# DeltaNet's z projection moves from the per-unit projections to the seven-product stage

## The chip, the cores and the metric

The kernel runs on one core of a Trainium2 chip. The time is the device time of one execution in microseconds (us). The engines are named as in the profile: PE (TensorE, matrix products), PEld (its weight loads), DVE (VectorE), ACT (ScalarE), POOL (GpSimd) and SP (SyncE, which here only issues DMAs). SPq and ACTq are the DMA issues on SP's and ACT's queues.

## The reference, cut to what matters

One layer, 512 tokens, 2048 channels, everything in float32:

```python
u = _rmsnorm(h, norm_w)
proj = jnp.matmul(u, w_in)            # 2048 x 20528
...
h_a = _mlstm_chunkwise(ml_q, ml_k, ml_v, i_pre, logf)      # 8 heads
h_a = _rmsnorm(h_a) * ml_norm_w * sigmoid(ml_o) * silu(ml_z)
qkv = _causal_conv_silu(dn_qkv, dn_conv_w)                  # width 4
h_b = _gated_delta_chunkwise(dq, dk_, dv_, beta, g)         # 16 heads of 128
h_b = _merge_heads(_rmsnorm(h_b, dn_norm_w)) * silu(dn_z)
y_a, y_b = h_a @ w_out[:2048], h_b @ w_out[2048:]
return sigmoid(gate_a) * y_a + sigmoid(gate_b) * y_b        # then residual, final norm
```

DeltaNet solves, per head and chunk, a unit lower triangular system, and then runs a chain over the chunks in which each state depends on the one before. The change concerns `dn_z`, the 2048 columns whose SiLU gates DeltaNet's normalised head outputs.

## The kernel before, in words

Each float32 operand is split into a high and a low part (`split_hi` on ACT, `split_lo` on DVE), and each product is three matmuls: high x high, high x low, low x high. The order of PE's instructions is the order in which the program is written; the other engines' and the DMA queues' order is made by a scheduler from dependences and priorities (`urgent`, `high_priority`, `behind`: not before the newest weight split).

The work outside the big products is written as generators that are advanced by `tick()`: after every step of a product loop, `tick` runs each generator whose due time has come, and `yield n` lets n steps pass. A step is six matmuls of 512 columns (twelve of 256 in `proj_tm`). So a PE instruction in a generator has a fixed place among the matmuls of the projections, and PE stands still there if its operand is not ready.

The stages are these.

1. Front. x is normalised and transposed into `uh`, `ul` (channels on partitions). Meanwhile the first mLSTM q and k blocks are projected and two blocks of output gates (`narrow_gates`). `u_sums` makes the sums of quarters of u that the next stage needs: POOL adds, ACT and DVE split, all in one tile `X`.
2. Seven-product stage, `seven`, nine blocks given by `SEVEN`. A block multiplies u by two times 512 columns of `w_in` with seven products in place of eight, in the manner of Strassen and Winograd: groups A and B of eight K steps each, with four and three products a step. `prep_sums` and `prep_pair` make and split the weights' sums. Blocks of kind z hold 512 columns each of mLSTM's z and o, kind v mLSTM's v, kind g output gates. `SINK` holds what is done with each kind's results: they come out token-major (tokens on partitions), pass an activation, and are stored to DRAM.
3. Units, in the order of `UNITS`: eight of DeltaNet (two heads each) and three of mLSTM, the first mLSTM unit (`ml_first`) running beside the first of them. `dn_unit` projects K, Q, V and z with `proj_cm`, 16 steps each, 64 in all; the results come channel-major. `conv_silu` and `silu_end` follow on ACT and DVE; `turn` transposes a tile in 32x32 blocks on DVE and by DMA through DRAM. `dn_front_k` makes the decay matrix and the triangular system and solves 32x32 blocks of it on DVE in 62 short instructions (L866, L868); the result goes through DRAM (`xd`, `tt`) and is transposed to `tn`. `dn_back`, started 9 steps after the last projection, combines the blocks on PE (its first product, L923, reads `tn`) and starts two `dn_chain`s, one per head, each some 20 steps long. At its end a chain normalises the head's outputs (`os`), turns them channel-major, and `gated` multiplies by the norm's weight and by `g`, the SiLU of z, on DVE, 13 steps later (`TURN`), and stores to `h_d`.
4. An mLSTM unit projects Q and K in 32 steps and runs `ml_prep`, `ml_rec` and `ml_fin` for two heads beside the following units. `ml_rec` scales `kw` on DVE just ahead of the products that read it (L1087, L1098).
5. Output: more gates, then `w_out` for mLSTM's part, then for DeltaNet's. `load_h` loads `hm_d` (kept in 32x32 blocks, scaled by the norm's weight when it is split) and `h_d` (channel-major, scaled already).

Buffers that the change's order touches: `wk` tiles have rings, shared by unit kinds: `g` 4, `kq` 4, `ke` 4, `aq` 4, `dm` 2, `to` 2; PSUM has three `pj`, three `wk` and two `o` banks. The weight loads of a unit run up to four tiles ahead (`RAHEAD`), the splits three (`SAHEAD`).

Of the kernel before, what the change touches and what calls it, by code (L numbers as in the profile page):

```python
# [8 lines left out]
F32 = mybir.dt.float32  # L9
# [23 lines left out]
KLAST = 4  # L33
TURN = 13
QWAIT = 9
# [21 lines left out]
def hybrid_body(  # L57
# [321 lines left out]
    def u_sums():  # L379
        for i in range(KH):  # L380
            uf, sf = X[:, 0, :, :], X[:, 1, :, :].rearrange("p a (b n) -> p (a b) n", n=HP)
            V.tensor_tensor(out=uf, in0=uh[:, 2 * i:2 * i + 2, :].bitcast(F32), in1=ul[:, 2 * i:2 * i + 2, :].bitcast(F32),
                            op=ALU.add)
            a11, a21, a12, a22 = uf[:, 0, 0:HP], uf[:, 0, HP:S], uf[:, 1, 0:HP], uf[:, 1, HP:S]
            G.tensor_tensor(out=sf[:, 0], in0=a21, in1=a22, op=ALU.add)
            G.tensor_tensor(out=sf[:, 1], in0=sf[:, 0], in1=a11, op=ALU.subtract)
            G.tensor_tensor(out=sf[:, 2], in0=a11, in1=a21, op=ALU.subtract)
            G.tensor_tensor(out=sf[:, 3], in0=a12, in1=sf[:, 1], op=ALU.subtract)
            yield 3
            for hi, lo, src in ((suh[:, i], sul[:, i], sf[:, 0:3]), (s4h[:, i], s4l[:, i], sf[:, 3])):  # L390
                A.copy(hi, src)
                V.tensor_tensor(out=lo, in0=src, in1=hi.bitcast(F32), op=ALU.subtract)
            yield 2

# [169 lines left out]
    def seven(n0, kind, c1, c2):  # L564
# [6 lines left out]
        def product(n, m):  # L571
            g, i = "AB"[n // KH], n % KH
            ps = ((m6, m1, m5, m7) if g == "A" else (m1, m5, m7))[m]
            hi, lo = partq[n0 + n][m]
            for t in range(2):
                ah, al = LHS[g][m](i, slice(t * P, (t + 1) * P))
                T.matmul(ps[t], ah, hi, start=(g == "A" and i == 0), stop=False, skip_group_check=True)  # L577
                T.matmul(ps[t], ah, lo, start=False, stop=False, skip_group_check=True)  # L578
                T.matmul(ps[t], al, hi, start=False, stop=(i == KH - 1), skip_group_check=True)  # L579
                if i == KH - 1 and ends[g][m] is not None:  # L580
                    ends[g][m](t)
            tick()

        N = 2 * KH
        for n in range(N - 2):
            prep_sums(n0 + n + 1)
            prep_pair(n0 + n + 1)
            load_quad()
            if n == N - 3:

                prep_sums(n0 + n + 3)
            for m in range(4 if n < KH else 3):
                if n == N - 3 and m == 2:
                    prep_sums(n0 + N - 1)
                    prep_pair(n0 + N - 1)
                product(n, m)

        load_quad()
        last = n0 + N == len(quads)
        for n, m in ((N - 2, 0), (N - 2, 1), (N - 1, 0), (N - 1, 1), (N - 2, 2), (N - 1, 2)):  # L600
            if (n, m) == (N - 1, 0):
                prep_pair(n0 + N)
                load_quad()
            if last and (n, m) == (N - 1, 1):
                limit[0] = len(plan)
                prepare(nfront - 1)
            product(n, m)
# [32 lines left out]
    def sink_z(c1, c2, m1, m5, m7, last):  # L640
# [31 lines left out]
        def end7(t):  # L672
# [3 lines left out]
        return end1, end5, end7  # L676

    SINK = {"g": sink_flat(lambda c, col: tg_d[c, :, col - GATE:col - GATE + NO], AF.Tanh, 0.5),
            "v": sink_flat(lambda c, col: v_d[c, :, col - ML_V:col - ML_V + NO], AF.Copy, 1.0),
            "z": sink_z}  # L680

# [72 lines left out]

    def silu2(ps, dst):
        th = wk.tile([P, S], F32, tag="th", name="thz", bufs=3)
        with urgent():
            A.copy(dst, ps)
        with urgent():
            A.activation(th, ps, AF.Tanh, scale=0.5)  # L760
        V.scalar_tensor_tensor(out=dst, in0=th, scalar=1.0, in1=dst, op0=ALU.add, op1=ALU.mult)

    def token_norms(pk, dst):
# [13 lines left out]
    def travel(o, dst, out):  # L777
# [10 lines left out]
        with behind("A") if out else urgent(2):  # L788
            q.dma_start(dst, d.rearrange("(n j) r a c -> (j r) n (a c)", n=NC))
        yield 1  # L790

    def gated(hn, w, g, kt):
        with behind("V"):
            V.scalar_tensor_tensor(out=g, in0=hn.rearrange("p c t -> p (c t)"), scalar=w, in1=g, op0=ALU.mult,
                                   op1=ALU.mult)
        nc.sync.dma_start(h_d[kt], g)
        yield 1
# [164 lines left out]
    def dn_chain(j, hs, kq, u):  # L962
# [7 lines left out]
        for c in range(NC):  # L970
# [18 lines left out]
            if c < NC - 1:  # L989
# [3 lines left out]
                with urgent():  # L993
                    if st is None:
                        V.tensor_copy(sn, pst)
                    else:
                        V.scalar_tensor_tensor(out=sn, in0=st, scalar=ge[:, c:c + 1], in1=pst,
                                               op0=ALU.mult, op1=ALU.add)
# [14 lines left out]
        with urgent():  # L1013
            V.tensor_tensor(out=os_, in0=po, in1=bc(rsd, P), op=ALU.mult)
        turn(os_, os_, True)
        start(gated(os_, normc[:, 32:33], u["g"][j], h), TURN)

    def dn_unit(p):
        hs = (2 * p, 2 * p + 1)
        dcol = p * NB  # L1020
        u = {"aq": [], "qt": [], "ke": [], "vs": [], "g": [], "dm": []}
        kq = [wk.tile([P, 2, S], F32, tag="kq", name=f"kq{h}", bufs=4) for h in hs]
# [16 lines left out]
        for j in range(2):  # L1039
# [3 lines left out]
            start(silu_end(vt.rearrange("p c t -> p (c t)"), (vt, vt)), 4 + 3 * j)  # L1043
        ps = proj_cm(DN_Z + dcol)
        for j in range(2):
            g = wk.tile([P, S], F32, tag="g", name="gz", bufs=4)
            silu2(ps[j], g)
            u["g"].append(g)
        start(dn_back(hs, kq, u), 9)

    def ml_prep(j, hs, kq, u):
# [26 lines left out]
        u["em"].append((w, we, de, qi))  # L1078

    def ml_rec(j, hs, kq, u):  # L1080
        h = hs[j]
# [3 lines left out]
        kw = u["kw"][j]  # L1085
        with behind("V"):
            V.tensor_tensor(out=kw, in0=kw, in1=bc(we, P), op=ALU.mult)  # L1087
        sq = wk.tile([P, NC], F32, tag="sq", name="sq")
        c1 = None
        for c in range(NC):  # L1090
# [57 lines left out]
    def ml_start(hs, kq, u):  # L1148
        for j in range(2):
            kw = wk.tile([P, NC, P], F32, tag="ke", name="kw", bufs=4)  # L1150
# [12 lines left out]
    def ml_first(hs, kq, u):  # L1163
# [4 lines left out]
        yield 4  # L1168
        with behind("V"):
            ml_start(hs, kq, u)  # L1170
        yield 5
        yield from ml_both(hs, kq, u)
# [23 lines left out]
    def load_h(base, step):  # L1196
        for k in range(KT):
            raw = wp.tile([P, S], F32, tag="wr", name="hr", bufs=NRAW)
            if base:
                nc.sync.dma_start(raw, h_d[k])  # L1200
                split_hi(hh[base][:, k, :], raw)
                split_lo(hl[base][:, k, :], raw, hh[base][:, k, :])
            else:

                w = normc[:, 16 + k:17 + k]
                nc.sync.dma_start(raw.rearrange("p (n t) -> p n t", n=NC),
                                  hm_d[k].rearrange("(n j) r a c -> (j r) n (a c)", n=NC))
                A.activation(hh[base][:, k, :], raw, AF.Copy, scale=w)
                V.scalar_tensor_tensor(out=hl[base][:, k, :], in0=raw, scalar=w, in1=hh[base][:, k, :].bitcast(F32),
                                       op0=ALU.mult, op1=ALU.subtract)  # L1210
            yield step
# [149 lines left out]
```

## Time and profile before

| | us |
|---|---|
| median of 3 runs | 2276.9 (2273.74 to 2278.14) |
| the profiled execution | 2278.73 |
| its span, first to last instruction | 2276.9 |
| front, to the first seven-product matmul | 136.4 |
| seven-product stage, 9 blocks | 136.4 to 842.0 |
| units | 842.0 to 1844.6 |
| output | 1844.6 to 2276.9 |

The granted clock of PE is 0.994 of full speed over the span. In a group's row stand the line, engine, operation, tiles, shape and count, then busy us, the mean ns of one, and the engine's idle time ahead of them with what ended it. A row of waits has who waited for whom, us in total, times, the longest. A timeline row has start, length, engine, line, operation and tiles, and in brackets the idle time before it. A row of stretches has the stretch, its length, the busy time and count of PE, PEld, DVE, ACT and POOL, PE's granted clock, the share of the DMA engines and GB/s.

### The profile page before, as it was taken

Reading aid. Unit: us, or ns where it says so; the run is one execution under the profiler, and the core shown is the slowest. Engines: PE = TensorE matmul, PEld = TensorE weight load, DVE = VectorE, ACT = ScalarE, POOL = GpSimd, SP = SyncE. Lnnn points to the kernel's source line nnn. Section 1 sums busy time; section 2 is a strip of 40 time slices with the busy share of each in tenths; the row PEclk is TensorE's granted clock in tenths of the full one; section 3 lists DMA queues with packets and bytes.
Section 4 is the critical chain, followed back from the end, with each engine's and each line's share of the span. In section 5 each row is a group of like instructions: output and inputs, shape, how many; then the busy total and the mean of one; then the engine's idle time right before and its main releaser. Section 6 shows DMA issues by size and latency. Waiting matters only on the chain.

```text
span 2276.9 us, 32977 instructions
## 1 busy us (share of the span) xinstructions
PE 2218.0 (97%) x11600; PEld 1858.0 (82%) x11600; DVE 1507.5 (66%) x2725; ACT 893.3 (39%) x1776; POOL 248.3 (11%) x325
## 2 busy tenths in 40 slices
PE   7999999999999999999999999999999999999998
PEld 5888888778778778788888888888888899978886
DVE  5967798777777757776496846867376855334445
ACT  4434444444444443343343434434334334232223
POOL 0500000000000001211021202212022100000111
PEclk9999999999999999999999999999999999999999
DMA  5366666667767757557565746658366556764333
GB/s 157 88 190 188 212 195 213 195 197 232 225 186 221 244 180 201 132 120 197 121 165 121 185 124 155 149 121 204 100 159 144 129 144 201 243 206 149 115 116 131
DMA packets 503464, 384.50 MB, mean 169 GB/s; under 512 B 238337, under 2 KB 402402, under 8 KB 503298
## 3 DMA queue, kind: packets, MB, share of 16 engines
q1 hardware_dynamic: 406018, 333.03, 52.5%
q10 hardware_dynamic: 97280, 49.37, 7.4%
q8 instruction: 91, 1.49, 0.3%
q14 instruction: 75, 0.61, 0.1%
HBM read 309.86 MB, written 72.42 MB: 168 GB/s over the span
## 4 chain that ended last, share of the span: by engine, by line
PE 75%; DMA 9%; DVE 8%; issue 3%; SPq 2%; ACT 1%; POOL 0%; ACTq 0%; DVEq 0%; POOLq 0%
PE pj L249 12%; PE pj L250 11%; PE pj L251 11%; PE ps L578 7%; PE ps L577 6%; PE ps L579 6%; PE py L1295 3%; PE py L1296 3%; PE py L1294 3%; DVE wl L138 3%; DMA wr<-in_w_in_dram 2%; DMA wr<-t_d 2%; PE pjt L264 2%; PE pjt L266 2%; PE pjt L267 2%
## 5 line engine op out<-in xcount | busy, mean ns | idle before, releaser
L138 DVE TENSOR_TENSOR wl<-wr,wh 128x512 fp32r<-128x512 f32 (+1 forms) x624 | 487.2, 786 | 346.0 <-ACT wh L135 336.0
L135 ACT CAST wh<-wr 128x512 fp32r<-128x512 f32 (+1 forms) x624 | 415.6, 669 | 760.3 <-PE pj L250 351.8
L249 PE MATMUL pj<-uh,wh 128*128 128x512 f32 x1280 | 531.1, 415 | 3.2 <-ACT yp L740 3.2
L251 PE MATMUL pj<-uh,wl 128*128 128x512 f32 x1280 | 501.8, 392 | 0.0
L250 PE MATMUL pj<-ul,wh 128*128 128x512 f32 x1280 | 501.3, 392 | 0.0
L251 PEld LDWEIGHTS pj<-uh,wl 128*128 128x128 f32 x1280 | 241.1, 188 | 53.0
L249 PEld LDWEIGHTS pj<-uh,wh 128*128 128x128 f32 x1280 | 242.0, 189 | 49.0 <-ACT yp L740 4.0
L250 PEld LDWEIGHTS pj<-ul,wh 128*128 128x128 f32 x1280 | 242.1, 189 | 43.1
L578 PE MATMUL ps<-wl,uh 128*128 128x512 f32 x432 | 170.6, 395 | 7.1 <-DVE wl L138 7.1
L577 PE MATMUL ps<-wh,uh 128*128 128x512 f32 x432 | 169.6, 393 | 2.5 <-DVE X L558 2.3
L579 PE MATMUL ps<-wh,ul 128*128 128x512 f32 x432 | 168.3, 390 | 0.0
L578 PE MATMUL ps<-wl,suh 128*128 128x512 f32 x432 | 168.1, 389 | 0.0
L577 PE MATMUL ps<-wh,suh 128*128 128x512 f32 x432 | 168.1, 389 | 0.0
L579 PE MATMUL ps<-wh,sul 128*128 128x512 f32 x432 | 168.1, 389 | 0.0
L264 PE MATMUL pjt<-wh,uh 128*128 128x256 f32 x512 | 149.1, 291 | 4.5 <-ACT tgs L696 2.7
L266 PE MATMUL pjt<-wl,uh 128*128 128x256 f32 x512 | 146.7, 287 | 0.4 <-DVE wl L138 0.4
L267 PE MATMUL pjt<-wh,ul 128*128 128x256 f32 x512 | 146.4, 286 | 0.0
L135 ACT CAST wh<-ts 128x512 fp32r<-128x512 f32 x144 | 88.9, 617 | 144.3 <-DVE ts L533 106.5
L135 ACT CAST wh<-t 128x1024 fp32r<-128x1024 f32 x72 | 75.8, 1053 | 160.7 <-PE ps L579 91.2
L138 DVE TENSOR_TENSOR wl<-ts,wh 128x512 fp32r<-128x512 f32 x144 | 98.2, 685 | 23.5 <-ACT wh L135 23.5
L138 DVE TENSOR_TENSOR wl<-t,wh 128x1024 fp32r<-128x1024 f32 x72 | 88.0, 1223 | 33.6 <-ACT wh L135 33.2
L578 PEld LDWEIGHTS ps<-wl,uh 128*128 128x128 f32 x432 | 81.1, 188 | 31.0 <-DVE wl L138 15.6
(286 smaller groups left out, 3691.8 us busy)
## 6 DMA issues: line engine op xcount, KB each, us to landing
wr<-in_w_in_dram SPq DMA_DIRECT2D x712, 256.0 KB, 3.5
wr<-in_w_out_dram SPq DMA_DIRECT2D x128, 256.0 KB, 3.1
t_d<-ts ACTq DMA_DIRECT2D x72, 256.0 KB, 3.7
wr<-t_d SPq DMA_DIRECT2D x72, 256.0 KB, 4.0
tgl<-tg_d SPq DMA_DIRECT2D x24, 256.0 KB, 3.6
xt<-in_x_dram SPq DMA_DIRECT2D x8, 512.0 KB, 7.4
v<-v_d SPq DMA_DIRECT2D x8, 512.0 KB, 5.9
gb<-rows_d SPq DMA_DIRECT2D x16, 256.0 KB, 4.1
```

The lines of the kernel that those rows point to most:

```text
L135: newest["A"] = A.copy(hi, src).ins
L138: newest["V"] = V.tensor_tensor(out=lo, in0=src, in1=hi.bitcast(F32), op=ALU.subtract).ins
L249: T.matmul(ps[j], hi[:, k, wsl], uh[:, kt, :], start=(kt == 0), stop=False)
L250: T.matmul(ps[j], hi[:, k, wsl], ul[:, kt, :], start=False, stop=False)
L251: T.matmul(ps[j], lo[:, k, wsl], uh[:, kt, :], start=False, stop=(kt == KT - 1))
L264: T.matmul(o, uh[:, kt, tsl], hi[:, k, :], start=(kt == 0 and c % 2 == 0), stop=False, skip_group_check=True)
L266: T.matmul(o, uh[:, kt, tsl], lo[:, k, :], start=False, stop=False, skip_group_check=True)
L267: T.matmul(o, ul[:, kt, tsl], hi[:, k, :], start=False, stop=(kt == KT - 1), skip_group_check=True)
L577: T.matmul(ps[t], ah, hi, start=(g == "A" and i == 0), stop=False, skip_group_check=True)
L578: T.matmul(ps[t], ah, lo, start=False, stop=False, skip_group_check=True)
L579: T.matmul(ps[t], al, hi, start=False, stop=(i == KH - 1), skip_group_check=True)
L1294: T.matmul(ps[c], hh[base][:, kt, tsl], hi[:, 0, :], start=(kt == 0), stop=False)
```

## The change

DeltaNet's z leaves `dn_unit`: the projection, `silu2` and `gated` go, and a unit has 48 steps. `SEVEN` gets two blocks of kind s, 1024 columns of z each, between kinds z and v (11 blocks). Their sink computes the SiLU (a copy and a tanh on ACT, one gating operation on DVE) and stores token-major to `gz_d`. A chain loads its head's part of `gz_d` on SP at its second chunk; POOL multiplies the normalised outputs by it, before they are turned; the turned blocks stay in `h_d` as they are, and `load_h` applies the norm's weight for both branches. `dn_back` starts 17 steps after V, where it started 9 after z.

Other steps move: `u_sums` uses two buffers and splits one round after the sums are made; `prep_sums` for the next block's first weights comes four products later; `scale_kw` is called a step before the first head's recurrence, and for the second head inside the first's; mLSTM's recurrence yields 3 in place of 4; `ml_first` starts its two heads five steps apart.

```diff
 SEVEN = ([("z", ML_Z + c, ML_O + c) for c in range(0, D, NO)]
+         + [("s", DN_Z + c, DN_Z + c + NO) for c in range(0, D, 2 * NO)]
          + [("v", ML_V + c, ML_V + c + NO) for c in range(0, D, 2 * NO)]
...
-    h_d = dr.tile([KT, P, S], F32, tag="hd", name="h_d")
+    h_d = dr.tile([KT, 16, BS, 4, BS], F32, tag="hd", name="h_d")
+    gz_d = dr.tile([NC, P, D], F32, tag="gzd", name="gz_d")
...
-        cols = (DN_K, DN_Q, DN_V, DN_Z) if kind == "d" else (ML_Q, ML_K)
+        cols = (DN_K, DN_Q, DN_V) if kind == "d" else (ML_Q, ML_K)
...
     def u_sums():
-        for i in range(KH):
...
-            yield 3
-            for hi, lo, src in ((suh[:, i], sul[:, i], sf[:, 0:3]), (s4h[:, i], s4l[:, i], sf[:, 3])):
-                A.copy(hi, src)
-                V.tensor_tensor(out=lo, in0=src, in1=hi.bitcast(F32), op=ALU.subtract)
-            yield 2
+        for i in range(KH + 1):
+            if i < KH:
+                sums(i)
+            yield 2
+            if i:
+                sf = sfs[i - 1]
+                for hi, lo, src in ((suh[:, i - 1], sul[:, i - 1], sf[:, 0:3]), (s4h[:, i - 1], s4l[:, i - 1], sf[:, 3])):
+                    A.copy(hi, src)
+                    V.tensor_tensor(out=lo, in0=src, in1=hi.bitcast(F32), op=ALU.subtract)
+            yield 3
...
+    def sums(i):
+        uf = sbp.tile([P, 2, NO], F32R, tag="w2h", name="uf", bufs=2).bitcast(F32)
+        sf = sfs[i] = X[:, i % 2, :, :].rearrange("p a (b n) -> p (a b) n", n=HP)
...
             load_quad()
-            if n == N - 3:
-
-                prep_sums(n0 + n + 3)
...
         for n, m in ((N - 2, 0), (N - 2, 1), (N - 1, 0), (N - 1, 1), (N - 2, 2), (N - 1, 2)):
+            if (n, m) == (N - 2, 1):
+                prep_sums(n0 + N)
...
+    def sink_s(c1, c2, m1, m5, m7, last):
+
+        def late(z, c, col):
+            th = spare(True)
+            with behind("A"):
+                A.activation(th, z, AF.Tanh, scale=0.5)
+            with behind("V"):
+                V.scalar_tensor_tensor(out=z, in0=th, scalar=1.0, in1=z, op0=ALU.add, op1=ALU.mult)
+            yield 2
+            with behind("A"):
+                nc.scalar.dma_start(gz_d[c, :, col - DN_Z:col - DN_Z + NO], z)
...
-    def gated(hn, w, g, kt):
-        with behind("V"):
-            V.scalar_tensor_tensor(out=g, in0=hn.rearrange("p c t -> p (c t)"), scalar=w, in1=g, op0=ALU.mult,
-                                   op1=ALU.mult)
-        nc.sync.dma_start(h_d[kt], g)
-        yield 1
...
             T.matmul(po[:, c, :], aq[:, c, 1, :], w, start=(st is None), stop=True)
+            if c == 1:
+                g = wk.tile([P, NC, P], F32, tag="g", name="gz", bufs=4)
+                nc.sync.dma_start(g, gz_d[:, :, h * P:(h + 1) * P].rearrange("c p n -> p c n"))
...
-        turn(os_, os_, True)
-        start(gated(os_, normc[:, 32:33], u["g"][j], h), TURN)
+        G.tensor_tensor(out=os_, in0=os_, in1=g, op=ALU.mult)
+        yield 2
+        turn(os_, h_d[h], True)
...
-        ps = proj_cm(DN_Z + dcol)
-        for j in range(2):
-            g = wk.tile([P, S], F32, tag="g", name="gz", bufs=4)
-            silu2(ps[j], g)
-            u["g"].append(g)
-        start(dn_back(hs, kq, u), 9)
+        start(dn_back(hs, kq, u), 17)
...
+    def scale_kw(j, u):
+        kw, we = u["kw"][j], u["em"][j][1]
+        with behind("V"):
+            V.tensor_tensor(out=kw, in0=kw, in1=bc(we, P), op=ALU.mult)
...
             if c == NC - 2:
+                if j == 0:
+                    scale_kw(1, u)
...
-            yield 4
+            yield 3
...
         for j in range(2):
             yield from ml_prep(j, hs, kq, u)
+        yield 5
+        scale_kw(0, u)
+        yield 1
...
-        with behind("V"):
-            ml_start(hs, kq, u)
-        yield 5
+        for j in range(2):
+            with behind("V"):
+                ml_start(hs, kq, u, (j,))
+            yield 5
...
-            if base:
-                nc.sync.dma_start(raw, h_d[k])
-                split_hi(hh[base][:, k, :], raw)
-                split_lo(hl[base][:, k, :], raw, hh[base][:, k, :])
...
+            w = normc[:, 32:33] if base else normc[:, 16 + k:17 + k]
+            nc.sync.dma_start(raw.rearrange("p (n t) -> p n t", n=NC),
+                              (h_d if base else hm_d)[k].rearrange("(n j) r a c -> (j r) n (a c)", n=NC))
```

More of the change, by code (lines that the diff above doesn't have):

```diff
@@ L579, in product @@
                 T.matmul(ps[t], al, hi, start=False, stop=(i == KH - 1), skip_group_check=True)
-                if i == KH - 1 and ends[g][m] is not None:
+                if i == KH - 1:
                     ends[g][m](t)
@@ L676, in sink_z, with out_, end5, end7 @@
         return end1, end5, end7
+    def sink_s(c1, c2, m1, m5, m7, last):
[8 more added lines that the diff above has]
+                nc.scalar.dma_start(gz_d[c, :, col - DN_Z:col - DN_Z + NO], z)
+        def out_(ps, t, col, wait):
+            z = spare(False)
+            with urgent(3):
+                A.copy(z, ps)
+            start(late(z, t, col), wait + 4 * t)
+        def end5(t):
+            add(m5[t], U1[t], m5[t])
+            out_(m5[t], t, c2, 5)
+        def end7(t):
+            add(U1[t], U1[t], m7[t])
+            start(late(U1[t], 2 + t, c1), 12 + 4 * t)
+            start(late(C22[t], 2 + t, c2), 14 + 4 * t)
+        return (lambda t: out_(m1[t], t, c1, 4)), end5, end7
     SINK = {"g": sink_flat(lambda c, col: tg_d[c, :, col - GATE:col - GATE + NO], AF.Tanh, 0.5),
             "v": sink_flat(lambda c, col: v_d[c, :, col - ML_V:col - ML_V + NO], AF.Copy, 1.0),
-            "z": sink_z}
+            "z": sink_z, "s": sink_s}
     def lead():
@@ L753, in silu_end @@
         yield 1
[L755 to L761, printed above, removed]
     def token_norms(pk, dst):
@@ L1146, in ml_both, with ml_start @@
             yield from ml_fin(j, hs, u)
-    def ml_start(hs, kq, u):
-        for j in range(2):
+    def ml_start(hs, kq, u, js=(0, 1)):
+        for j in js:
             kw = wk.tile([P, NC, P], F32, tag="ke", name="kw", bufs=4)
@@ L1168, in ml_first @@
         yield 4
-        with behind("V"):
-            ml_start(hs, kq, u)
-        yield 5
+        for j in range(2):
+            with behind("V"):
+                ml_start(hs, kq, u, (j,))
+            yield 5
         yield from ml_both(hs, kq, u)
@@ L1198, in load_h @@
             raw = wp.tile([P, S], F32, tag="wr", name="hr", bufs=NRAW)
-            if base:
-                nc.sync.dma_start(raw, h_d[k])
-                split_hi(hh[base][:, k, :], raw)
-                split_lo(hl[base][:, k, :], raw, hh[base][:, k, :])
[L1203 to L1210, printed above, removed]
+            w = normc[:, 32:33] if base else normc[:, 16 + k:17 + k]
+            nc.sync.dma_start(raw.rearrange("p (n t) -> p n t", n=NC),
+                              (h_d if base else hm_d)[k].rearrange("(n j) r a c -> (j r) n (a c)", n=NC))
+            A.activation(hh[base][:, k, :], raw, AF.Copy, scale=w)
+            V.scalar_tensor_tensor(out=hl[base][:, k, :], in0=raw, scalar=w, in1=hh[base][:, k, :].bitcast(F32),
+                                   op0=ALU.mult, op1=ALU.subtract)
             yield step
```

20 lines of the change are left out of this document (9 added, 11 removed).

## The prediction

> **What bounds the kernel now.** I read the page's busy table and slices first, then what TensorE (PE) waited for, then the start times of single matmuls, then busy times by stretch, and last the order of single instructions in one DeltaNet unit.
>
> ```profile
> PE 2218.0 (97%) x11600; PEld 1858.0 (82%) x11600; DVE 1507.5 (66%) x2725; ACT 893.3 (39%) x1776; POOL 248.3 (11%) x325
> PE   7999999999999999999999999999999999999998
> ```
> ```profile
> PE pprm L103 <- POOL rs L315: 14.8, 1, 14.8
> PE ps L578 <- DVE wl L138: 7.1, 12, 1.4
> PE pcs L1098 <- DVE kw L1087: 4.4, 3, 3.4
> PE pj L249 <- ACT yp L740: 3.2, 2, 2.3
> PE pjt L264 <- ACT tgs L696: 2.7, 1, 2.7
> PE pjt L264 <- ACT qk L360: 1.9, 1, 1.9
> ```
> PE is busy from end to end. After the first 14.8 us its largest single waits are 3.4, 2.7 and 2.3 us. So the time is the sum of what PE issues, plus whatever waits the change takes away or makes. The first question is what one matmul costs.
>
> ```profile
> 1560.28 0.39 PE L249 MATMUL pj<-uh,wh 128*128 128x512 f32 x1
> 1560.51 0.39 PE L250 MATMUL pj<-ul,wh 128*128 128x512 f32 x1
> 1560.74 0.39 PE L251 MATMUL pj<-uh,wl 128*128 128x512 f32 x1
> ```
> Each lasts 0.39 us, but the next starts 0.227 us later: they overlap, and 0.227 us is the price. The Trainium skill, TensorE: Matmul & The Clock Gate, section "Wait — 56ns, not 53.3ns?", gives N over 2.4 GHz plus about 2.5 ns from start to start, 0.2157 us at 512 columns; the trace shows 5% more and decides. With the page's figure the PE term below would be 96 x 0.2157 = 20.7 us in place of 21.8.
>
> **The projections.** One step (tick) of the hand-written order is six matmuls, 6 x 0.227 = 1.36 us. These are the four projections of one DeltaNet unit (K, Q, V, z) and the one after it:
>
> ```profile
> 1478.90:1505.00 26.10, 26.10 (x210) 20.93 (x209) 13.23 (x21) 8.62 (x17) 4.99 (x11) 1.00 0.54 128
> 1505.00:1534.60 29.60, 29.60 (x165) 25.49 (x164) 21.62 (x54) 11.84 (x29) 6.49 (x7) 1.00 0.45 108
> 1534.60:1560.30 25.70, 25.70 (x132) 21.70 (x131) 23.12 (x62) 8.82 (x29) 5.55 (x8) 1.00 0.80 195
> 1560.30:1582.00 21.70, 21.70 (x97) 18.00 (x96) 19.23 (x52) 11.22 (x31) 1.63 (x2) 1.00 0.86 225
> 1582.00:1608.10 26.10, 26.10 (x209) 20.90 (x209) 9.80 (x15) 8.68 (x18) 4.61 (x11) 1.00 0.52 140
> ```
> The columns are length, PE, weight loads, DVE, ACT, POOL, each with its count. The z projection is 96 matmuls and nothing else: 96 x 0.227 = 21.8 us. The attention products that fill the other three stay, wherever they go. The change removes eight such blocks: **-174.4 us**.
>
> **The seven-product blocks.** A block multiplies 1024 columns by 8 steps x 7 products x 2 x 3 = 336 matmuls, where projections would take 384. By issue alone two blocks cost 672 x 0.227 = 152.5 us. As run, the first and the last of the four z/o blocks and the first v block:
>
> ```profile
> 136.40:214.20 77.80, 77.10 (x339) 62.87 (x338) 56.20 (x70) 32.78 (x46) 0.00 (x0) 1.00 0.63 195
> 369.10:447.30 78.20, 77.49 (x338) 62.69 (x337) 63.84 (x83) 35.97 (x53) 0.00 (x0) 1.00 0.64 202
> 447.30:527.00 79.70, 77.67 (x338) 62.52 (x336) 63.59 (x83) 34.66 (x52) 0.00 (x0) 1.00 0.67 197
> ```
> Four z/o blocks take 447.3 - 136.4 = 310.9, 77.7 each; the v block takes 79.7. A new s block has the DVE work of a z/o block (8 gating operations on 128x512, the same sums and splits), two ACT operations more (ACT is busy 36 of 78), and eight stores of 256 KB on ACT's queue in place of four. So 2 x 77.7 = **+155.4 us** (bounds 152.5 and 159.4). Net of both terms: **-19.0 us**.
>
> **DMAs.** Each unit loses eight 256 KB weight loads and two h stores on SP's queue, and two reads back on ACT's. It gains two reads of the gated z on SP, like the reads of g_d that mLSTM heads issue now:
>
> ```profile
> mg<-g_d SPq DMA_DIRECT2D x16, 256.0 KB, 4.0
> h_d<-gz SPq DMA_DIRECT2D x16, 256.0 KB, 3.1
> ```
> Such a read is issued some 12 steps (16 us) before it is used, four times its 4.0 us. If its buffer were not free, the weight loads queued behind it on SP would be late; they run four tiles ahead, 4 x 2.72 = 10.9 us, and that is the cover. I cost the DMAs at nothing. The two s blocks add the loads of any seven block, during which the DMA engines stand at 0.63 to 0.67. At the end, the scaling of h_b moves into load_h as it stands for h_a: the same number of ACT and DVE operations, nothing.
>
> **Steps given out elsewhere.** In the front, ACT copies the sums of u as soon as POOL makes them:
>
> ```profile
> 110.34 0.83 ACT L391 CAST suh<-X 128x768 fp32r<-128x768 f32 x1 [1.66 <-POOL X L386]
> 111.91 0.59 ACT L696 ACTIVATE tgs<-pjt 128x512 f32<-128x512 f32 x1
> ```
> The eviction tgs stands behind that copy, and PE waits 2.7 us for it (first waits above). With two buffers and the copy one round later, POOL is done long before: **-2.7 us** (bounds 0 and -4.6, with the wait on qk). The scaling of kw is given out one step (first head) or a chunk (second head) earlier: of the 4.4 us I take **-4.0** (bounds 0 and -4.4). The next block's first sums come four products later, so they no longer stand ahead of the last weights of the block; part of the 7.1 us on wl goes, over eleven blocks: **-2.0** (bounds -4 and +2, if the next block's first weights come late instead).
>
> **Where it can give back: the 48-step unit.** Now the DVE solves a triangular system per unit, link by link, and PE uses the result much later. Rows of the same unit, in order of time; V ends at 1560.30:
>
> ```profile
> 1538.39 0.19 DVE L866 TENSOR_TENSOR tmp<-ls,xi 128x31 f32<-128x31 f32 x1 [1.06 <-DMA ls<-ld]
> 1580.04 0.17 DVE L868 TENSOR_TENSOR xi<-xi,tmp 128x8 f32<-128x8 f32 x1
> 1581.74 2.52 SPq L876 DMA_DIRECT2D xd<-xi  x4
> 1585.76 0.37 SPq L877 DMA_DIRECT2D tt<-xd  x1
> 1589.04 0.45 DVE L880 STREAM_TRANSPOSE tn<-tt 128x256 f32<-128x256 f32 x1 [5.68 <-DMA tt<-xd]
> ```
> ```profile
> 1594.37 0.41 PE L923 MATMUL p<-tn,aq 32*32 32x32 f32 x14
> ```
> The solve ends 19.9 us after V, tn is ready at 1589.49, 29.2 us after V. PE asks at 1594.4: z's 16 steps and 9 more gave it 34.1 us. After the change PE asks 17 steps after V, 17 x 1.36 = **23.2 us**. The DVE cannot simply hurry: over V and z it is busy 23.1 + 19.2 of 47.4 us. Two more units, by the end of V and tn:
>
> ```profile
> 1009.80:1035.50 25.70, 25.70 (x132) 21.70 (x131) 22.67 (x62) 8.66 (x28) 5.57 (x8) 1.00 0.76 183
> 1066.66 0.45 DVE L880 STREAM_TRANSPOSE tn<-tt 128x256 f32<-128x256 f32 x1 [6.92 <-DMA tt<-xd]
> 1689.60:1717.20 27.60, 26.42 (x125) 21.58 (x123) 24.43 (x59) 8.40 (x18) 7.06 (x6) 1.00 0.68 154
> 1744.83 0.45 DVE L880 STREAM_TRANSPOSE tn<-tt 128x256 f32<-128x256 f32 x1 [4.84 <-DMA tt<-xd]
> ```
> tn is 31.6 and 28.1 us after V there. Two things shift it. The chain of the previous unit ran in steps 18 to 38 and will run in 26 to 46, so 8 of its 20 steps move from Q into V. Q and V hold 68 + 35 extra PE records in 7.9 + 4.0 us, 0.115 us each; 68 of them per unit are the chain's (17 products, two heads, two records each), so 8/20 x 68 x 0.115 = 3.1 us: V ends that much later against the solve. And DVE work ahead of the solve's end changes: the two gating operations leave DVE (-1.7 us), some six chain operations of 0.35 us move in (+2.1). That is even within half a us.
>
> ```profile
> L794 DVE SCALAR_TENSOR_TENSOR gz<-os,normc,gz 128x512 f32<-128x512 f32 x14 | 11.8, 843 | 0.0
> L979 DVE SCALAR_TENSOR_TENSOR r<-pr,negeg,vt 128x128 f32<-128x128 f32 x42 | 14.7, 350 | 29.4 <-PE pr L976 29.0
> ```
> So tn stands at 29.2 - 3.1 = 26.1 (31.6 - 3.1 = 28.5 in the earliest) against 23.2. Where an mLSTM unit follows (three times) its first 16 steps hold nothing else on PE, and it stalls 2.9, 2.9 and 5.3 us. Where a DeltaNet unit follows, the last mLSTM products stand before the ask, which leaves 28.1 - 3.1 - 23.2 = 1.8 or less; I take 0 for those, and 1.5 each for the first and the last unit. Together **+14 us** (bounds: 0, if the solve ends six us sooner; 45, below). Once late, the next links keep their distance of two steps, so the stall is paid once a unit.
>
> **Sum.** -19.0 - 2.7 - 4.0 - 2.0 + 14 = -13.7 us. The profiled execution took 2278.7 us, of which its span is 2276.9; 2278.7 - 13.7 = 2265.0, and the median of the three runs shown lies 1.8 below it: **2263 us**.
>
> **Rivals.** (B) *Every deadline holds*: the solve is not late, +14 falls away, 2276.9 - 27.7 = 2249. For it: DVE is busy only 13 of 26 us in K, so work put there costs nothing. Against it: the solve sits in V, where DVE is full. (C) *The solve is late by its present distance and more, slower*: POOL now multiplies the heads' outputs by z near step 46, in the midst of the solve. What that does to the solve:
>
> ```profile
> 1552.78 1.29 POOL L893 TENSOR_TENSOR kq<-kq,gb 128x512 f32<-128x512 f32 x1
> 1552.93 1.23 DVE L868 TENSOR_TENSOR xi<-xi,tmp 128x66 f32<-128x66 f32 x1
> 1555.53 0.23 DVE L868 TENSOR_TENSOR xi<-xi,tmp 128x63 f32<-128x63 f32 x1
> ```
> A link that meets a POOL multiply takes 1.23 instead of 0.23 us; two such a unit add 2 us. With them, and V's end unshifted, tn stands 6 us late where mLSTM follows (8.4 in the earliest) and 4.9 elsewhere: 6 + 6 + 8.4 + 5 x 4.9 = 45 us, 2276.9 - 27.7 + 45 = 2294. It decides from 27.7 / 8 = 3.5 us a unit on. The Trainium skill, GPSIMD Engine Reference, section "1. Specifications", says that its SBUF interfaces are shared with VectorE, with contention when a DVE instruction has two SBUF inputs; the two rows agree, and by that rule the change puts the gating on the worse engine. (D) *No change that shows*: the chain's links in V each come late. There are 16 chains of six DVE links; a convolution ahead of a link takes 0.75 us, which a distance of two steps mostly covers; at 0.15 us each they cost 96 x 0.15 = 14 more, 2277. Against it, the only wait of PE on such a link today:
>
> ```profile
> PE pr L976 <- DVE st L997: 1.0, 1, 1.0
> ```
>
> **How the numbers follow.** Chances: forecast 0.42 (own range 2256 to 2271), B 0.25, C 0.20, D 0.13. About 0.2% (4.6 us) is what a measurement tells from no change. Forecast and B are faster beyond it: 0.67, and a little of D: 0.68; the same 0.12, slower 0.20. The range reaches past B's 2249 by the outer bounds of the small terms, and up into C, not to its full price: 2246 to 2288.
>
> **What would show it.** Eleven blocks of 77 to 79 us and DeltaNet units 22 us shorter confirm the first term. tn later than PE's ask by 2 to 5 us before mLSTM units, and PE's list of waits led by p on tn, confirm the second; no such row means B, six us or more in all units C. A wait of PE on kw or tgs as now would refute the small terms. The forecast is wrong as a whole if s blocks take well over 80 us, or if a new wait (on a buffer, or on SP's reads of z) heads PE's list.

## The result, and the profile after

The changed kernel takes 2336.9 us (median; 2336.3 to 2339.5) against 2275.3 (2268.6 to 2278.1) of the kernel before beside it: a ratio of 1.0277, 95% interval 1.0252 to 1.0302. It is slower by about 62 us, where 2263 was forecast. The profiled execution's span grew from 2276.9 to 2335.6, by 58.7 us.

The busy table and slices of the profile after come first, then the waits of PE:

```profile
PE 2215.2 (95%) x11504; PEld 1849.5 (79%) x11504; DVE 1590.3 (68%) x2793; ACT 912.0 (39%) x1788; POOL 263.5 (11%) x341
PE   7799999999999999999879998999899999989998
PEclk9899999999999999999989999999999999999999
```
```profile
PE p L946 <- DVE tn L903: 41.2, 8, 13.3
PE pprm L104 <- POOL rs L316: 14.5, 1, 14.5
PE prf L462 <- DVE sml L449: 9.1, 1, 9.1
PE ps L588 <- DVE wl L139: 6.0, 10, 1.7
...
PE pk L849 <- DVE kq L788: 4.2, 5, 1.1
PE pnum L1119 <- DVE xi L891: 4.1, 3, 1.6
```
Eights and a seven now stand among the nines in the second half of PE's slices. PE has 96 matmuls fewer, which is 96 x 0.227 = 21.8 us, yet its busy time fell by only 2.8 (2218.0 to 2215.2): 19.0 us of stretched matmuls. Its idle time doubled, from 2276.9 - 2218.0 = 58.9 to 2335.6 - 2215.2 = 120.4, by 61.5 us. Together 61.5 + 19.0 - 21.8 = 58.7, the whole difference. Of the idle time, 41.2 us is p on tn, which before the change had no row, and 9.1 is prf on sml, a row that is new too. The waits on kw and tgs are gone.

The stages of the changed kernel (front, seven-product stage, units, output), in a view by stretches with the columns known from the prediction:

```profile
0.00:148.10 148.10, 117.19 (x705) 102.42 (x706) 98.29 (x148) 60.34 (x101) 37.26 (x48) 0.94 0.42 123
148.10:1006.50 858.40, 848.33 (x3699) 690.56 (x3698) 675.73 (x854) 385.32 (x556) 0.00 (x0) 1.00 0.67 208
1006.50:1895.70 889.20, 832.00 (x4622) 689.18 (x4621) 620.09 (x1487) 331.30 (x872) 193.94 (x265) 0.97 0.60 146
1895.70:2335.60 439.90, 417.63 (x2485) 367.35 (x2483) 196.15 (x306) 135.05 (x261) 32.27 (x29) 0.98 0.52 160
```
Against the stage times before, the front lost 148.1 - 136.4 = 11.7 us. The seven-product stage grew by 858.4 - 705.6 = 152.8. The units shrank by 1002.6 - 889.2 = 113.4 instead of 174.4: 61.0 of the gain is missing there. The output took 439.9 for 432.3; the last unit's stall on tn lies in it, because a unit now ends with V.

The unit that the prediction worked with, the sixth DeltaNet unit, in order of time. V ends at 1663.1 now (1560.3 before). The rows are of DVE, SP's queue and PE:

```profile
1680.88 0.17 DVE L891 TENSOR_TENSOR xi<-xi,tmp 128x8 f32<-128x8 f32 x1
1682.14 0.76 SPq L819 DMA_DIRECT2D vt<-td  x1
1683.54 0.57 SPq L899 DMA_DIRECT2D xd<-xi  x1
1684.62 0.37 SPq L819 DMA_DIRECT2D vt<-td  x1
1685.04 0.56 SPq L899 DMA_DIRECT2D xd<-xi  x1
1686.29 1.21 SPq L899 DMA_DIRECT2D xd<-xi  x2
1689.61 0.37 SPq L900 DMA_DIRECT2D tt<-xd  x1
1692.11 0.45 DVE L903 STREAM_TRANSPOSE tn<-tt 128x256 f32<-128x256 f32 x1 [5.96 <-DMA tt<-xd]
1692.70 0.53 PE L946 MATMUL p<-tn,aq 32*32 32x32 f32 x12 [6.35 <-DVE tn L903]
```
The solve does end earlier against V, 1681.05 - 1663.1 = 18.0 us after it where it was 19.9. But the hand-over through DRAM, from the solve's end to the end of tn, takes 11.5 us where it took 9.3 (1589.49 - 1580.21): the four xd writes, one stretch of 2.52 us before, start 1 us later behind the solve and are spread over 4 us, with a read of the turned v ahead of them and one between them on the same queue. So tn is 29.5 us after V, against an ask at 29.6 - 6.35 = 23.2.

After such a stall the matmuls are slow. The second DeltaNet unit, PE's timeline:

```profile
1222.00 1.06 PE L946 MATMUL p<-tn,aq 32*32 32x32 f32 x32 [13.35 <-DVE tn L903]
...
1223.59 0.63 PE L251 MATMUL pj<-ul,wh 128*128 128x512 f32 x1
1224.02 0.63 PE L252 MATMUL pj<-uh,wl 128*128 128x512 f32 x1
```
They start 0.43 us apart in place of 0.227. The view by stretches, over the seven stretches of the units in which the granted clock is 0.5 (two of them and their sum):

```profile
1211.60:1228.60 17.00, 6.60 (x53) 4.95 (x56) 3.97 (x17) 1.37 (x3) 3.08 (x11) 0.50 0.21 46
...
1604.10:1607.50 3.40, 3.40 (x10) 2.62 (x9) 3.40 (x7) 0.27 (x1) 2.03 (x4) 0.50 0.81 224
...
sum 51.00, PE 31.05 PEld 24.35 DVE 17.07 ACT 7.01 POOL 17.77; mean PE 4.44 PEld 3.48 DVE 2.44 ACT 1.00 POOL 2.54
```
Work that is done at the half clock loses 1 - 0.227/0.43 = 0.47 of its time. Taking this share for all of the work, as an estimate, 31.05 x 0.47 = 14.6 us. In the units before the change there were two such stretches:

```profile
868.40:871.80 3.40, 3.40 (x14) 3.01 (x13) 3.40 (x6) 0.90 (x3) 1.08 (x2) 0.50 1.04 277
929.90:936.70 6.80, 5.84 (x14) 4.64 (x15) 6.06 (x14) 1.92 (x5) 0.00 (x0) 0.50 0.82 154
```
Their 9.24 us of work lost 4.3, so the clock took 10.3 us more from the units than before. Two stretches in the output with 6.6 us of work took another 3.1. That leaves 5.6 of the 19.0 us of stretched matmuls; they were not taken apart.

### The profile page after: what moved, and what is told of

It reads as the page before. It is cut to its first block, busy times and chain, and to the rows that moved or that the text cites. A ratio compares the mean times of both kernels' runs of the same rounds, so it can differ in the third digit from the quotient of the medians.

```text
span 2335.6 us, 32926 instructions
## 1 busy us (share of the span) xinstructions
PE 2215.2 (95%) x11504; PEld 1849.5 (79%) x11504; DVE 1590.3 (68%) x2793; ACT 912.0 (39%) x1788; POOL 263.5 (11%) x341
## 4 chain that ended last, share of the span: by engine, by line
PE 29%; DMA 9%; DVE 7%; issue 2%; SPq 2%; ACT 1%; ACTq 0%; DVEq 0%; POOL 0%; POOLq 0%
PE pj L250 5%; PE pj L251 4%; PE pj L252 4%; PE py L1321 3%; PE py L1322 3%; PE py L1320 3%; DVE wl L139 2%; DMA hr<-h_d 1%; DMA wr<-in_w_out_dram 1%; PE pjt L265 1%; DVE tmp L889 1%; PE pjt L267 1%; PE pjt L268 1%; DVE xi L891 1%; DMA xd<-xi 1%
## 5 line engine op out<-in xcount | busy, mean ns | idle before, releaser
L250 PE MATMUL pj<-uh,wh 128*128 128x512 f32 x1024 | 434.8, 425 | 2.0 <-ACT yp L778 2.0
L252 PE MATMUL pj<-uh,wl 128*128 128x512 f32 x1024 | 407.1, 398 | 4.7 <-DVE wl L139 4.7
L251 PE MATMUL pj<-ul,wh 128*128 128x512 f32 x1024 | 405.5, 396 | 0.0
L252 PEld LDWEIGHTS pj<-uh,wl 128*128 128x128 f32 x1024 | 195.5, 191 | 50.0 <-DVE wl L139 6.0
L250 PEld LDWEIGHTS pj<-uh,wh 128*128 128x128 f32 x1024 | 196.4, 192 | 38.4 <-ACT yp L778 2.8
L251 PEld LDWEIGHTS pj<-ul,wh 128*128 128x128 f32 x1024 | 196.8, 192 | 34.0
L588 PE MATMUL ps<-wl,uh 128*128 128x512 f32 x528 | 208.1, 394 | 6.4 <-DVE wl L139 6.0
L587 PE MATMUL ps<-wh,suh 128*128 128x512 f32 x528 | 205.7, 390 | 0.6 <-ACT to L627 0.5
L589 PE MATMUL ps<-wh,ul 128*128 128x512 f32 x528 | 205.7, 390 | 0.0
L588 PE MATMUL ps<-wl,suh 128*128 128x512 f32 x528 | 205.5, 389 | 0.0
```

Source lines behind the costliest of these rows:

```text
L250: T.matmul(ps[j], hi[:, k, wsl], uh[:, kt, :], start=(kt == 0), stop=False)
L251: T.matmul(ps[j], hi[:, k, wsl], ul[:, kt, :], start=False, stop=False)
L252: T.matmul(ps[j], lo[:, k, wsl], uh[:, kt, :], start=False, stop=(kt == KT - 1))
```

## The experiments

Ratios are to the kernel before on the same chip, with 95% intervals; a ratio step of 0.01 is 22.7 us. In the kernels with the sums of u as before, line numbers are 9 lower from `prep_sums` on.

**The sums of u as before.** `u_sums` of the kernel before, the rest as changed:

```diff
-        for i in range(KH + 1):
-            if i < KH:
-                sums(i)
-            yield 2
...
+        for i in range(KH):
+            uf, sf = X[:, 0, :, :], X[:, 1, :, :].rearrange("p a (b n) -> p (a b) n", n=HP)
...
+            yield 3
```


> The changed kernel with u_sums as it was before (one buffer, split right after POOL's sums). Theory (in the front the double-buffered sums of u crowd the 38 dependent links of the gate arithmetic on DVE, so that prf waits 9.1 us): the wait of prf on sml goes, the front ends at about 136 us instead of 148, the whole is 10 to 14 us shorter than the changed kernel, about 2324 us; units and their waits on tn stay (41 us). Rival (the front is longer for another reason, such as the later order of loads): no change beyond 3 us.

Measured: 1.0200 [1.0174, 1.0226], 2313.9 us, 17.5 less by the ratio. Its waits of PE:

```profile
PE p L937 <- DVE tn L894: 39.3, 7, 13.3
...
PE pjt L265 <- ACT tgs L725: 2.7, 1, 2.7
```
The wait of prf is gone, that of tgs is back at 2.7, and the first seven-product matmul starts at 136.9 in place of 148.1. So the double-buffered sums save 2.7 us on ACT, and with them the front ends some 11 us later; what is above 11 us of the 17.5 isn't in the front, and since the two intervals leave 9 to 26 us it may be noise. These rows of the changed kernel (DVE and PE) show where:

```profile
105.03 0.22 DVE L452 SCALAR_TENSOR_TENSOR sml<-sml 128x64 f32<-128x64 f32 x1
105.17 0.38 PE L462 MATMUL prf<-ident,sml 128*8 128x128 f32 x1 [9.05 <-DVE sml L449]
```
```profile
87.83 0.21 DVE L442 SCALAR_TENSOR_TENSOR sml<-sml 128x64 f32<-128x64 f32 x1
```
The second fence is the same operation of the kernel before (L442 there): the gates' chain of short dependent DVE operations ended at 88.0 us and now ends at 105.2. The sums' DVE operations stood between the chain's links before as well, but spread out until 113.1 us; the edit has all of them done by 102.0, ahead of the chain's last links. Undone, the wait goes.

**The rest of the unit eight steps later.**

```diff
-        start(dn_back(hs, kq, u), 17)
+        start(dn_back(hs, kq, u), 25)
```


> The changed kernel with dn_back started 25 steps after V instead of 17, as far behind V as it was before the change. Theory (PE asks for tn before the solve has delivered it, and each stall is followed by a stretch at half clock): all but the second unit's stall on tn go (of 41.2 us at most 8 stay), the half-clock stretches in the units go with them, together 45 to 60 us less than the changed kernel: 2277 to 2292. Rival (DVE has no room for a unit of 48 steps, so the lateness moves to the chain's links or to the next unit's buffers): the waits on tn go but others of 30 us or more come, and the time stays above 2310.

Measured: 1.0076 [1.0054, 1.0097], 2285.1 us: 46 less than the changed kernel. PE's largest wait behind that on pprm:

```profile
PE pk L849 <- DVE kq L788: 11.1, 5, 3.6
```
The stall on tn is down to 0.6 us. The distance of `dn_back` from V is most of the loss. It isn't free: pk now waits 11.1 us for kq. That the later links meet the next unit's key work on DVE is argued, not shown; that the wait goes with the distance is seen below.

**The kernel before, with the ask eight steps earlier.** Nothing of the change but its place: `dn_back` 1 step after z, which is 17 after V.

```diff
-        start(dn_back(hs, kq, u), 9)
+        start(dn_back(hs, kq, u), 1)
```


> The kernel before, with dn_back started 1 step after z, that is 17 steps after V, and nothing else changed. Theory (the place of the ask alone makes the stall): tn comes 27 to 32 us after V as now, the ask about 23 to 26 us after V; PE stalls on tn 2 to 9 us a unit, 30 to 50 us in all, with half-clock stretches behind them: 2275 + 40 to 65 = 2315 to 2340. Rival (the stall needs the shorter unit, DVE having more room with z in it, so that the order made for the earlier ask brings tn earlier too): under 15 us in all, 2290 or less.

Measured: 1.0245 [1.0222, 1.0267], 2323.6 us.

```profile
PE p L923 <- DVE tn L880: 33.0, 7, 7.6
```
The place alone, in a unit of 64 steps with z still in it and the gating still on DVE, costs some 55 us by the ratio and 49.2 by the profiled spans (2326.1 - 2276.9). Of these, 33.0 are the stall, and the half clock behind it, worked out as above, is some 14 more. Neither the shorter unit nor the new work on POOL is needed for the loss.

**Gating on DVE in place of POOL.**

```diff
-        G.tensor_tensor(out=os_, in0=os_, in1=g, op=ALU.mult)
+        V.tensor_tensor(out=os_, in0=os_, in1=g, op=ALU.mult)
```


> The changed kernel with the multiplication of the heads' outputs by z on DVE instead of POOL. Theory A (POOL's multiplications lengthen the solve through the port they share with DVE): the solve ends 1 to 2 us sooner after V in each unit, the waits on tn fall by 8 to 16 us, 2315 to 2328. Theory B (the solve's end is set by the sum of DVE work ahead of it, and 0.7 us of DVE work is as dear as what the POOL operation costs): tn and the total within 5 us of the changed kernel.

Measured: 1.0244 [1.0222, 1.0267], 2324.0 us, 7.5 less than the changed kernel, of which the two intervals leave 0 to 15.

```profile
PE p L946 <- DVE tn L903: 40.9, 8, 13.8
```
The stall is the same without POOL's multiplies. Yet they do slow the solve a little. In the changed kernel four of the sixteen, in four of the units, slow one operation of the solve each (POOL and DVE, the sixth unit; the solve's operations beside it take 0.20):

```profile
1664.23 1.28 POOL L1041 TENSOR_TENSOR os<-os,gz 128x512 f32<-128x512 f32 x1 [0.75 <-DVE os L1040]
```
```profile
1664.30 1.28 DVE L889 TENSOR_TENSOR tmp<-ls,xi 128x49 f32<-128x49 f32 x1
```
With the gating on DVE this unit's solve ends 16.8 us after V in place of 18.0, but the hand-over takes 12.4 in place of 11.5, and tn comes at 29.3 in place of 29.5. So rival C's mechanism is there, at one operation in four of the eight units in place of two in each, and it does not decide the stall.

**Both heads of the first mLSTM unit at once.** `ml_first` as before the change:

```diff
-        for j in range(2):
-            with behind("V"):
-                ml_start(hs, kq, u, (j,))
-            yield 5
+        with behind("V"):
+            ml_start(hs, kq, u)
+        yield 5
```


> The changed kernel with one edit: the first mLSTM unit starts both heads at once, as before the change. Theory (the second DeltaNet unit's late tn, 38.5 us after V, comes from the ring of four aq buffers: the mLSTM heads now let go of one 11 us after DeltaNet asks for it): the wait of 13.35 us on tn in the second unit and the 17.1 us at half clock behind it go for the most part; tn there comes 30 to 33 us after V, the view of waits shows p on tn at 28 to 34 us in place of 41.2; 15 to 25 us less than the changed kernel. Rival (that unit is late because its solve meets more DVE work, like the others, only more of it): tn stays at 36 us or more, the wait stays over 11 us, the time moves by less than 5 us.

Measured: 1.0184 [1.0167, 1.0201], 2311.2 us, 21 less. The second DeltaNet unit and the sum of the waits:

```profile
1200.34 0.87 PE L946 MATMUL p<-tn,aq 32*32 32x32 f32 x25 [5.29 <-DVE tn L903]
```
```profile
PE p L946 <- DVE tn L903: 27.5, 8, 6.9
```
The 13.35 us stall is 5.29, near those of the two other units ahead of an mLSTM unit (6.91 and 6.17 in this run), and tn comes 28.4 us after V there in place of 38.5. The first unit's stall falls too, from 5.78 to 1.83. `v1` of mLSTM and `aq` of DeltaNet share a ring of four; with the heads started five steps apart, mLSTM's first unit held a buffer that the second unit's matrix needed:

```profile
1137.83 0.68 DVE L851 TENSOR_TENSOR aq<-pk,dm 128x512 f32<-128x512 f32 x1
...
1148.65 0.70 DVE L804 STREAM_TRANSPOSE to<-v 128x512 f32<-128x512 f32 x1
...
1149.70 0.68 DVE L851 TENSOR_TENSOR aq<-pk,dm 128x512 f32<-128x512 f32 x1
```
The two rows of L851 are the two heads' first operations on aq in the changed kernel, 11.9 us apart, the second right behind the last turning of mLSTM's results out of `v1`; with both heads started at once they are 1.2 us apart (1130.08 and 1131.25). The solve starts after both.

**Three edits together, at 25, 21, 23 and 19 steps.** The sums of u as before, both first heads at once, and `dn_back` at the distance given; at 25 also with the gating on DVE. 21 was run twice.

```diff
-        start(dn_back(hs, kq, u), 17)
+        start(dn_back(hs, kq, u), 21)
```


> The changed kernel with three edits undone or moved: the sums of u as before, the rest of the DeltaNet unit started 25 steps after V (the distance before the change), the first mLSTM unit's heads started at once. If the three losses add (17.5 for the sums by the first comparison, about 46 for the place, and of the ring only what 25 steps still leave, 0 to 6): 2262 to 2272 by the before kernel's 2269 of the batch before, so no slower than before. If they overlap (the late gates chain and the late units are the same clock loss): 2275 or more.

> As the kernel with three edits, but the rest of the unit starts 21 steps after V. Asks come 5.4 us earlier than at 25 steps, at about 31 to 33 us after V's end, with tn ready at 27 to 31 where nothing disturbs it: p waits on tn in at most three units, under 8 us in all. If later links stay out of the next unit's key norms this way, the wait of pk on kq (11.1 us with 25 steps) falls to 4 to 6 us and the time is 3 to 8 us below the 25-step kernel; if tn is late again it is 5 to 20 us above.

> As the kernel with three edits at 25 steps, with the heads' outputs multiplied by the gated z on DVE in place of POOL. If POOL's multiplies slow DVE's links through a shared port, 3 to 10 us less than with POOL; if only the length of the single links changes and no wait hangs on it, within 3 us of it.

> The three edits (sums of u as before, both heads of the first mLSTM unit at once, the rest of the DeltaNet unit moved), with 19 steps after V in place of 21. With 21, PE's ask stands 29.3 us after V's end in the odd units with tn ready at 24.0 to 25.2, and 31.7 to 32.0 in the others with tn at 26.8 to 28.3 (first unit 37.9 and 35.1). Two steps fewer are 2.7 us: tn is just in time everywhere but in the first unit; if tn stays where it is, the time is within 4 us of the kernel with 21. If the solve slows again as the chain of the unit before moves back under V (tn at 28 or later in the odd units), p waits on tn at 8 us or more and it is 8 us or more above.

> As the kernel with 21 steps, with 23. If what costs with 25 steps is the links that run on into the next unit's key norms (pk waits on kq 12.5 us there, none with 21), some of it shows here: 3 to 10 us above the kernel with 21. If only the place of tn counts, it is the same as with 21, within 3 us.

> The kernel with 21 steps once more, beside its neighbours on one chip and with more rounds: 0.996 to 1.0 of the kernel before; the lowest of the three if the place has its best between 19 and 23.

| steps after V | ratio to before | median us | p on tn, us | pk on kq, us |
|---|---|---|---|---|
| 19 | 1.0120 [1.0098, 1.0142] | 2296.0 | 19.5 | none |
| 21 | 0.9980 [0.9968, 0.9991] | 2265.6 | none | none |
| 21, again | 0.9979 [0.9967, 0.9991] | 2263.2 | none | none |
| 23 | 0.9983 [0.9970, 0.9996] | 2265.4 | none | 3.7 |
| 25 | 1.0037 [1.0022, 1.0052] | 2278.6 | none | 12.5 |
| 25, gating on DVE | 1.0028 [1.0010, 1.0045] | 2276.0 | none | 10.7 |

At 21 and 23 steps the kernel is faster than before by 0.2%. The order between them isn't settled (the 3 to 10 us more that were expected at 23 do not show), and the gating's engine makes no difference that shows. At 25 steps the three gains did not add: 8.9 us below the kernel at 25 steps with the new sums, not 17.5 and more. With 19 steps tn was to be just in time, or else the solve slower and 8 us or more lost: 32 us were lost, by the ratios on one chip, and mostly not in the solve. Its fourth DeltaNet unit on SP's queue (V ends at 1397.7), and then the same unit with 21 steps (V ends at 1388.8):

```profile
1410.89 1.24 SPq L890 DMA_DIRECT2D xd<-xi  x2
...
1413.65 3.07 SPq L805 DMA_DIRECT2D td<-to  x4
...
1423.07 0.56 SPq L890 DMA_DIRECT2D xd<-xi  x1
...
1426.03 0.37 SPq L891 DMA_DIRECT2D tt<-xd  x1
```
```profile
1400.26 1.22 SPq L890 DMA_DIRECT2D xd<-xi  x2
...
1402.64 1.28 SPq L890 DMA_DIRECT2D xd<-xi  x2
...
1409.80 0.46 SPq L891 DMA_DIRECT2D tt<-xd  x1
```
The solve ends 13.2 us after V with 19 steps and 11.4 with 21. But with 19 the last xd writes stand behind the turning of v, so tt is read 15.1 us after the first write instead of 9.5, and PE waits 5.1 us. In the second, fourth, sixth and eighth unit alike the solve ends 1.6 to 1.8 us later and the hand-over takes 4.3 to 4.8 us longer: the order of the DMAs makes most of the lateness, DVE the smaller part.

The place of `dn_back` thus moves the solve as well as the ask. In the fourth unit it ends 17.9 us after V at 17 steps (the changed kernel), then 13.2, 11.4, 11.0 and 9.5 at 19, 21, 23 and 25, and at 25 with nothing else changed 9.6. Why it ends sooner the later `dn_back` starts, no run shows.

**The stalls filled with work.** The changed kernel, and ahead of the products that wait for tn as many unread products as fit into each unit's stall:

```diff
+FILL = [48, 112, 21, 57, 11, 53, 6, 33]
...
         p1 = psw.tile([P, 2 * NC, BS], F32, tag="wk", name="p1")
+        for _ in range(FILL[hs[0] // 2]):
+            T.matmul(p1.rearrange("p a b -> p (a b)"), uh[:, 0, 0:P], uh[:, 0, 0:HP], start=True, stop=True)
```


> The changed kernel with work added: ahead of the products that wait for tn, PE gets 48, 112, 21, 57, 11, 53, 6 and 33 products of 128x256 in the eight DeltaNet units, which nobody reads; at 0.12 us each they are 40.9 us and fill the 41.2 us that PE stood waiting there. Theory (the clock falls to half because PE stood idle): the view of waits shows p on tn at under 8 us, the half-clock stretches of the units fall from 51 us to under 15, and the time falls by 10 to 20 us below the changed kernel although PE has more to do. Rival (the clock falls for another reason, or the half-clock stretches cost nothing): the stretches stay near 50 us, or they go and the time stays within 4 us of the changed kernel.

Measured: 1.0236 [1.0216, 1.0256], 2322.4 us. By the ratio it is 9.3 us faster than the changed kernel (the two intervals leave some 2 to 17), a little under what was expected. The added products and what is left of the stall:

```profile
L945 PE MATMUL p<-uh 128*128 128x256 f32 x341 | 42.1, 283 | 0.0
```
```profile
PE p L949 <- DVE tn L904: 3.0, 4, 1.4
```
```profile
1003.10:1879.30 876.20, 856.37 (x4929) 717.61 (x4928) 618.41 (x1484) 331.47 (x871) 194.05 (x264) 1.00 0.60 148
```
PE does 42.1 us more, its stall is 38.2 shorter, and the units' granted clock is 1.00 in place of 0.97: one stretch of 3.4 us at half clock is left of 51, so that 27.6 us less work runs at it, 27.6 x 0.47 = 13.0. The two stretches in the output are gone as well, 3.1 more. Together 42.1 - 38.2 - 13.0 - 3.1 = -12.2 us, inside the 2 to 17 that the intervals leave. So the half clock here comes of PE's standing still, since more work takes it away, and its cost is of the size worked out above.

## Why the prediction was wrong

**The bound and the price of a matmul** held: the whole difference comes out of PE's issue, its idle time and its clock.

**z out of the units, -174.4, and s blocks, +155.4**, held. The seven-product stage grew by 152.8 us. With no stall on tn, at 21 steps, the units take 837.1 us (991.7 to 1828.8), 165.5 less than before, though on another chip.

**kw (-4.0), tgs (-2.7), block sums (-2.0).** The waits on kw and tgs went as forecast, and ps on wl fell from 7.1 to 6.0. But "POOL is done long before: -2.7 us (bounds 0 and -4.6)" looked at ACT only. The edit moves the sums' DVE operations too, past the gates' chain that PE needs next: the front got longer by 11.7 us, outside the bounds and of the other sign.

**The stall on tn, +14**, is the step that failed. The ask at 23.2 us after V was right to a tenth. "So tn stands at 29.2 - 3.1 = 26.1" was not: the 3.1 us that V moves were given back, 1.2 by the solve and 2.2 by the hand-over, whose DMAs share SP's queue with the turning of v and were taken as a fixed length. The working also held the solve's end fixed but for the 3.1 us, while the runs at 19 to 25 steps show that it moves with the place of `dn_back`. In the units ahead of an mLSTM unit the stall was 6.82 and 6.35 for 2.9. The second DeltaNet unit had 13.35 for 5.3: `ml_first`'s stagger stood in the diff and was costed at nothing, though `aq` is a ring that both kinds of unit share. In the units ahead of a DeltaNet unit, taken as 0, tn is 27.0 to 29.9 us after V against asks of 26.3 to 27.6: 0.8, 1.5 and 2.6 us. First and last unit: 5.78 and 3.96 for 1.5 each. In all 41.2.

**What a stall costs beyond itself** was missing. The forecast took 1 us of stall as 1 us of time. The half clock adds 10.3 us in the units and 3.1 behind them, and the filled kernel shows that it is real. 41.2 - 14 = 27.2 of stall, 11.7 + 2.7 = 14.4 in the front and these 13.4 are 55.0 of the 72.4 us between the forecast's -13.7 and the measured +58.7. Waits in the units that have rows only after the change (pk on kq 4.2, pnum on xi 4.1) are 8.3 more; the remaining 9 were not taken apart.

**The rivals.** C gave nearly the stall that came, 45 us, but by luck: the gating on DVE left the stall at 40.9. Its 3.5 us a unit from which the change loses was exceeded by 41.2 / 8 = 5.2. B is what 21 steps and the two other edits come near to: no stall, but only 5 us gained where it gave 28; links of `dn_back` behind tn that come late (p on ta 8.2, p on s 6.7 us in the second run) take some, much as D supposed of the chain's links, and the rest stays open. The range ended at 2288, because its upper end was C's price cut short, and no case had two losses at once.

## What to carry to other kernels

When the work that hides a latency moves away, move the consumer with it, and find its new place by trying: from 21 steps, two earlier cost 32 us here, two later nothing that shows, and four later 13. Price a hand-over with the DMA queue as it will be, and check each ring and each in-order engine that a moved step passes, in the small "free" edits above all. On PE, price a stall at more than its length.

## What the runs showed of the hardware that was not expected

Short waits were enough for the half clock: the 3.40 us at 0.50 from 1604.1 on, in the stretches above, begin 1.2 us after a wait of 1.48 us, in a stage where PE is otherwise full:

```profile
1602.88 0.69 PE L946 MATMUL p<-tn,aq 32*32 32x32 f32 x32 [1.48 <-DVE tn L903]
```
The half-clock stretches are 3.4 us or near multiples of it. They also start on one grid: 1211.60 and 1604.10 are 392.5 us apart, 115 times 3.413, and the 868.40 and 929.90 of the kernel before 61.5, 18 times 3.417. The Trainium skill, TensorE: Matmul & The Clock Gate, Part 1, gives two clocks, full and half, and a free-running window of about 3.4 us; the stretches agree with both. Its section "HAM oscillation — how this bites in real kernels" tells of idle gaps of over some 3.4 us as what brings the half clock; here it came after a wait of 1.48 us, and the measurement decides.

The length of the wait alone does not decide, though. These are two stretches of the same grid in the changed kernel, each 3.4 us long. The first, with the wait of 1.48 us, came just before the half clock; the second has a longer wait, and the clock stayed full:

```profile
1600.70:1604.10 3.40, 1.92 (x39) 1.33 (x38) 1.72 (x3) 0.26 (x1) 1.82 (x5) 1.00 0.52 116
1194.50:1197.90 3.40, 1.68 (x8) 1.15 (x7) 3.40 (x6) 2.13 (x10) 0.83 (x1) 1.00 0.61 127
1197.90:1201.30 3.40, 3.40 (x17) 2.71 (x16) 3.40 (x9) 2.44 (x8) 0.00 (x0) 1.00 0.94 200
```
```profile
1196.54 0.50 PE L252 MATMUL pj<-uh,wl 128*128 128x512 f32 x1 [1.72 <-DVE wl L139]
```
PE was busy for more of the first stretch than of the second, but 0.69 us of it were the 32x32 products on tn, while the second holds only products of 128x512. That such small products count for less is a guess that fits both; no run here tests it.
